# A shared scores bank returned by its last reader, buffers counted, values behind four pairs' queries, the small loads held, level tiles of 32x32

## The chip, the cores and the metric

The kernel runs on one core of one Trainium2 chip. The number that counts is the time of one execution on the device, in microseconds (us). Before the change the median of three runs is 564.14 us.

## The reference, cut to what matters

One layer of a decoder trunk on 512 positions of width 1024, batch 1, all in float32:

```python
h = rmsnorm(x, norm1_w)
proj = h @ w_in                    # one projection, columns split among three groups
y_a = dilated_attention(aq, ak, av, bias_a)      # A: 6 heads of 64, three (window, dilation) branches
y_b = gla(bq, bk, bv, br, ba, ...)               # B: 4 heads, keys of 32, values of 64, decay gate of rank 16
y_c = moba_attention(cq, ck, cv, bias_c)         # C: 6 heads of 64, blocks of 256, top 3 of the past
mix = concatenate([y_a, y_b, y_c])
x = x + mix @ w_out
h2 = rmsnorm(x, norm2_w)
x = x + square(relu(h2 @ w_ff1)) @ w_ff2         # w_ff1 is 1024 x 4096
return rmsnorm(x, final_norm_w)
```

At 512 positions the three dilated branches of a query reach known sets of keys, so the kernel computes A as one softmax with an added table (relative bias and the logarithm of how many branches hold the distance), and C as one causal softmax with a bias: two blocks of 256 leave nothing to choose. In B, log a = log_sigmoid(a_lr @ w_a2 + b_a) / 16 is the decay, and o_t = q_t S_t with S_t = diag(a_t) S_(t-1) + k_t v_t.

## The kernel before

**Precision.** Weights and activations of the large products are split into a high and a low part in the rounded float32 format that TensorE multiplies in one pass (fp32r). `wh` is the rounded weight, made on ScalarE, `wl = w - wh`, made on VectorE; `xh` and `xl` are the same for the activations. A product is three matmuls: high by high, high by low, low by high. A matmul in plain fp32 is two passes and leaves two records in the trace.

**Stages.** The projection runs in pieces. `first()` (L753) streams eight slices of x (`xT`, 128 x 512) and of `w0` (128 x 528), and sums B's queries and keys (`bq`, `bk`) and B's values with the gate's low-rank input (`av`) over them. `qk_proj(p)` (L1183) makes queries and keys of a pair p of heads, A's and C's twelve heads being six pairs: two weight pieces per pair, 24 products each, into `qkps`. `v_proj()` (L1114) makes A's and C's values, `out_proj()` (L1349) the output projection, `ffn()` (L1570) the feed-forward part in units; these three use seven products of half-size sums in place of eight (`f1X`, `f2Z` and the like are their accumulators). `main()` (L1640) runs them in this order, with the values behind the queries of two pairs.

Beside them go `row_scale()` (L636): sums of squares over the slices, `rsp`, then `ss`, `rstd`, `diag` on VectorE and `rps` on TensorE, which spreads 1/rms along the rows. `bias_table()` (L666) multiplies the relative biases by a one-hot table: `vt`, then `vals`, written to DRAM as `tab`. `gla()` (L770): `alps` transposes the gate input to `alT`, `zps` multiplies it by w_a2, and a scan gives the decay. The 128 x 128 causal blocks of B are computed by levels: at level L (64, 32, ... 1), queries in the later half of each group of 2L positions meet keys in the earlier half, with a decay measured from the point between. The level products `lp` are four heads in four strips of 32 rows of TensorE, for four chunks n of 128 positions: the 128 columns of keys are loaded as weights, 64 columns of queries stream, for every level, and the entries outside a level are thrown away afterwards: levels 64 and 32 by ScalarE copies of the valid rows, the rest by a masked copy on VectorE. `attention()` (L952) makes the scores of one pair (`sps`), with 64 rows of TensorE for each head; `softmax()` (L1055) reads a bank of scores into `P` and normalises; `values()` (L1025) transposes P and multiplies it by the values.

**What sets the order.** The order of instructions on every engine is worked out when the program is built. Each part is a stream of operations; `Plan` (L107) holds a clock for each engine, gives every operation an estimated cost (L43 on), and issues next the operation with the earliest start, ties by the stream's priority and age. A stream can wait for an event, or take one of a resource. Resources are the eight PSUM banks (two `mm` for the large products, two `s`, two `pt`, one `o`, one `g`), the weight buffers, and so on. `slot()` (L227) hands out 52 small SBUF buffers of 2 KB per partition (`SLOTS`); the plan doesn't know about these, so an operation whose buffer is not yet free waits on the chip although the plan saw no wait.

`SCORES` and `HOMES` are tables: into which blocks the scores of a pair's four query blocks are cut, and which banks each takes. Pairs 2, 3 and 4 run query block 3 first (six matmuls) and then the three others (eighteen). Query block 0 shares the bank of block 2 (`SHARED`); the bank is given back by the softmax of the block that is last in the list.

`load_small()` (L624) issues the small constants on GpSimd's queue once the second slice's `xh` is made: `cst` (identity, flip and mask), `smask`, `hsel`, `rb` (relative bias), `bav`, `wa2`, `oneh`, then `lmask` and `gw`. All helpers record their operations on one line, L136 (L171 after the change), so the rows are told apart by their tiles' names.

Of the kernel before, what the change touches and what calls it, by code (L numbers as in the profile page):

```python
# [19 lines left out]
NT = S // 128  # L20
# [11 lines left out]
SCORES = {0: ((3, 2, 0, 1),), 1: ((3, 2, 0, 1),), 2: ((3,), (2, 0, 1)), 3: ((3,), (2, 0, 1)), 4: ((3,), (2, 0, 1)), 5: ((3,), (2, 0), (1,))}  # L32
SHARED = {(p, 0): 2 for p in range(6)}
HOMES = {0: {3: ('s', 's'), 2: ('o', 'g'), 1: ('pt', 'pt')}, 1: {3: ('s', 's'), 2: ('o', 'g'), 1: ('pt', 'pt')}, 2: {3: ('s', 's'), 2: ('s', 's'), 1: ('o', 'g')}, 3: {3: ('s', 's'), 2: ('s', 's'), 1: ('o', 'g')}, 4: {3: ('s', 's'), 2: ('s', 's'), 1: ('o', 'g')}, 5: {3: ('s', 's'), 2: ('s', 's'), 1: ('s', 's')}}
O_ORDER = (0, 1, 3, 5, 2, 4, 6)
# [4 lines left out]
class Op:  # L40


    def __init__(self, eng, method, args, kw):  # L43
# [14 lines left out]
        if eng == "tensor":  # L58
# [4 lines left out]
            elif wide and inner[-1].shape[0] == 32:  # L63
                self.cost = 0.031
# [9 lines left out]
        elif eng == "vector":  # L74
# [4 lines left out]
            self.cost = 0.075 + n * rate / 1000  # L79
        elif eng == "gpsimd":  # L80
            self.cost = 0.15 + n * (0.9 if method == "memset" else 2.1) / 1000
        if method == "dma_start":
            self.cost = 0.9 if "accum_op" in kw else 0.06
            self.rate = 170e3 if "accum_op" in kw else 320e3
            self.size = 4 * n * args[0].shape[0]

# [20 lines left out]
class Plan:  # L107
# [5 lines left out]
    def __init__(self, nc, resources):  # L113
        self.nc = nc
        self.clock = dict(tensor=0.0, scalar=0.0, vector=0.0, gpsimd=0.0, sync=0.0, dge=0.0, dma=0.0)
# [7 lines left out]
    def spawn(self, gen, prio=0):  # L123
        self.streams.append(dict(gen=gen, prio=prio, item=None, at=self.now, sent=None, n=len(self.streams)))
# [7 lines left out]
    def start(self, op, at):  # L132
        return max([self.clock[op.eng], at] + [self.ready.get(n, 0.0) for n in op.ins])

    def issue(self, op, at):
        getattr(getattr(self.nc, op.eng), op.method)(*op.args, **op.kw)  # L136
        t = self.start(op, at)
        end = t + op.cost
# [4 lines left out]
        if op.method == "dma_start":  # L143
            if "accum_op" in op.kw:
                self.clock["dma"] = max(self.clock["dma"], end + 1.0) + op.size / op.rate
                end = self.clock["dma"] + 3.0
            else:
# [3 lines left out]
        for n in op.outs:  # L151
            self.ready[n] = max(self.ready.get(n, 0.0), end + self.LAT)
        return end
# [7 lines left out]
    def run(self):  # L161
        while self.streams:
            cand, moved = None, False
            for st in list(self.streams):
                while True:
                    if st["item"] is None:
                        try:
                            moved = True
# [27 lines left out]
                    if cand is None or (t, st["prio"], st["n"]) < cand[:3]:  # L196
                        cand = (t, st["prio"], st["n"], st, o)
# [15 lines left out]
def hybrid_block_kernel(ctx: ExitStack, tc: tile.TileContext, xT_d, x_d, w0_d, wv_d, wqk_d, wo_d, w1_d, w2_d,  # L213
                        nw_d, ba_d, wa2_d, gw_d, fw_d, rb_d, oh_d, cst_d, lm_d, out_d):
# [8 lines left out]
    plan = Plan(nc, dict(BANKS, raw=3, rawv=5, rawo=8, w=WPAIRS, big=BIGS, raw2=3, part=5, lev=4, xp=2))  # L223
# [3 lines left out]
    def slot(name, dt=F32, shape=(128, 512)):  # L227
        return sp.tile(list(shape), dt, name=name, tag="slot", bufs=SLOTS)
# [34 lines left out]
    rb, wa2, gw = misc[:, 0:128], misc[:, 128:256], misc[:, 256:512]  # L263
    lmask = slot("lmask", I32, (128, len(LEVELS), 64))
    oneh = [slot("oneh", shape=(128, 320)) for _ in range(2)]
    alT = slot("alT", shape=(128, 512))
    xT = [slot("xT") for _ in range(KT)]
    tab = dr.tile([12, 640], F32, name="tab")
    R, Rn8, ssx = slot("R"), slot("Rn8"), slot("ssx")
# [354 lines left out]
    def load_small():  # L624
        yield ("wait", ("xh", 1))
        for t, d in ((cst, cst_d[:, 0:512]), (smask, cst_d[:, 512:1024]), (hsel, cst_d[:, 1024:1028]), (rb[:34, :12], rb_d),
                     (bav, ba_d), (wa2[:16], wa2_d)):
            yield POOL.dma_start(t, d)
        for i in range(2):
            yield POOL.dma_start(oneh[i][:34], oh_d[:, i * 320:(i + 1) * 320])  # L630
        fire("consts")
        spawn(bias_table(oneh), 1)
# [33 lines left out]
    def bias_table(oneh):  # L666
        yield ("wait", "R")
        for i in range(2):
# [1104 lines left out]
```

## Time and profile before

| | |
|---|---|
| three timed runs | 564.91, 564.14, 563.35 us |
| median | 564.14 us |
| profiled execution | 565.38 us |
| its span, first to last instruction | 563.4 us |
| mean TensorE clock granted | 0.998 |
| ScalarE, VectorE, GpSimd busy | 370.9, 478.9, 68.9 us |
| moved by DMA | 96.59 MB, mean 171 GB/s |

The profile is one execution. PE is TensorE, PEld its weight loads, which overlap the matmuls, DVE is VectorE, ACT ScalarE, POOL GpSimd. A row of a group names `out<-in`, the count, busy time, the mean of one in ns, and the idle time of the engine just before with what ended it. Matmuls are pipelined, so the time of one record is longer than the distance from its start to the next one's; distances are what counts. The span leaves out some 2 us around the first and the last instruction.

### The profile page before, as it was taken

What the parts mean: (1) busy time and instruction counts of PE and PEld (TensorE: products, weight loads), DVE (VectorE), ACT (ScalarE), POOL (GpSimd) and SP (SyncE); (2) the same over time, 40 slices, a digit from 0 to 9 for tenths busy, and PEclk for the clock granted to TensorE, in tenths of its full rate; (3) what the DMA queues carried; (4) which work ended last, traced back from release to release, by engine and by line L of the source; (5) the groups of instructions that cost most, each with busy time, mean ns of one, the idle gap of its engine ahead of it and who ended that gap; (6) DMA issues with size and microseconds to landing.
All of it is one profiled execution on the core that took longest, in us unless ns stands there. A gap on an engine that the chain in (4) does not pass through costs nothing.

```text
span 563.4 us, 9466 instructions
## 1 busy us (share of the span) xinstructions
PE 552.7 (98%) x3513; PEld 477.5 (85%) x3513; DVE 478.9 (85%) x872; ACT 370.9 (66%) x661; POOL 68.9 (12%) x90
## 2 busy tenths in 40 slices
PE   8999999999999999999999999999999999999994
PEld 7977887886876767899987899988999888999884
DVE  4899899998668988999699995799957899867984
ACT  5755745787665866989766476855377654679553
POOL 5003110001000002111121010120020110102102
PEclk9999999999999999999999999999999999999999
DMA  8944596195134756992989439686388694385803
GB/s 280 403 139 116 91 267 165 33 390 140 38 47 136 244 137 126 266 273 65 282 202 200 157 80 290 188 149 192 113 177 272 121 219 146 89 211 113 149 37 113
DMA packets 29949, 96.59 MB, mean 171 GB/s; under 512 B 3648, under 2 KB 3690, under 8 KB 29904
## 3 DMA queue, kind: packets, MB, share of 16 engines
q0 software_dynamic: 9456, 33.53, 32.9%
q1 hardware_dynamic: 20160, 62.20, 31.0%
q8 instruction: 27, 0.44, 0.3%
q10 hardware_dynamic: 288, 0.27, 0.1%
q14 instruction: 18, 0.15, 0.1%
HBM read 93.86 MB, written 2.13 MB: 170 GB/s over the span
## 4 chain that ended last, share of the span: by engine, by line
PE 81%; DVE 11%; DMA 3%; ACT 2%; issue 2%; SPq 0%; DVEq 0%; ACTq 0%; POOLq 0%
PE f2X L136 14%; PE f1X L136 13%; PE qkps L136 9%; PE f1Z L136 8%; PE f2Z L136 7%; PE ops L136 7%; PE f1Y L136 4%; PE vps L136 4%; DMA wraw<-in_w 3%; PE f2Y L136 3%; DVE wl L136 3%; PE ptp L136 3%; PE po L136 2%; PE sps L136 2%; DVE P L136 2%
## 5 line engine op out<-in xcount | busy, mean ns | idle before, releaser
L136 DVE TENSOR_TENSOR wl<-wraw,wh 128x1024 fp32r<-128x1024 f32 (+2 forms) x174 | 192.1, 1111 | 37.0 <-ACT wh L136 36.8
L136 ACT ACTIVATE wh<-wraw 128x1024 fp32r<-128x1024 f32 (+2 forms) x173 | 164.2, 966 | 58.2 <-DMA wraw<-in_w 14.6
L136 PE MATMUL f1X<-yp,wh 128*128 128x256 f32 x512 | 92.7, 283 | 0.0
L136 PEld LDWEIGHTS f1X<-yp,wh 128*128 128x128 f32 x512 | 80.1, 192 | 0.3
L136 POOL DMA_DIRECT2D wraw<-in_w x46 | 40.5, 947 | 270.0 <-DVE wl L136 220.1
L136 PE MATMUL f1X<-yp,wl 128*128 128x256 f32 x256 | 72.4, 283 | 0.0
L136 PE MATMUL f2X<-wh,Al 128*128 128x512 f32 (+1 forms) x132 | 50.6, 383 | 0.0
L136 PE MATMUL f2X<-wh,Ah 128*128 128x512 f32 (+1 forms) x132 | 50.5, 383 | 0.0
L136 PE MATMUL f2X<-wl,Ah 128*128 128x512 f32 (+1 forms) x132 | 50.5, 383 | 0.0
L136 PEld LDWEIGHTS f1X<-yp,wl 128*128 128x128 f32 x256 | 49.1, 192 | 0.0
L136 PE MATMUL f1Z<-yp,wh 128*128 128x256 f32 x256 | 46.3, 283 | 0.0
L136 ACT ACTIVATE h<-h 128x512 f32<-128x512 f32 x56 | 34.7, 625 | 10.5 <-DVE h L136 9.9
L136 PE MATMUL qkps<-xh,wh 128*128 128x512 f32 x96 | 40.3, 420 | 0.0
L136 PEld LDWEIGHTS f1Z<-yp,wh 128*128 128x128 f32 x256 | 39.9, 192 | 0.0
L136 ACT ACTIVATE Ah<-h 128x512 fp32r<-128x512 f32 x40 | 24.1, 620 | 21.5 <-DVE h L136 21.5
L136 PE MATMUL qkps<-xh,wl 128*128 128x512 f32 x96 | 37.6, 392 | 0.0
L136 PE MATMUL qkps<-xl,wh 128*128 128x512 f32 x96 | 37.4, 390 | 0.0
L136 PE MATMUL f1Z<-yp,wl 128*128 128x256 f32 x128 | 36.2, 283 | 0.0
L136 ACT ACTIVATE P<-P,mn 128x512 f32<-128x512 f32 (+3 forms) x48 | 26.4, 552 | 7.9 <-DVE mn L136 7.9
L136 DVE TENSOR_TENSOR Al<-h,Ah 128x512 fp32r<-128x512 f32 x40 | 26.9, 688 | 3.2 <-ACT Ah L136 3.0
L136 PEld LDWEIGHTS f2X<-wh,Ah 128*128 128x128 f32 x132 | 24.8, 188 | 4.9
L136 PEld LDWEIGHTS f2X<-wl,Ah 128*128 128x128 f32 x132 | 24.8, 188 | 4.8
(264 smaller groups left out, 1221.0 us busy)
## 6 DMA issues: line engine op xcount, KB each, us to landing
wraw<-in_w SPq DMA_DIRECT2D x66, 512.0 KB, 5.3
wraw<-in_w POOLq DMA_DIRECT2D x46, 512.0 KB, 6.8
wraw<-in_wqk SPq DMA_DIRECT2D x12, 512.0 KB, 6.7
wraw<-in_wv SPq DMA_DIRECT2D x10, 512.0 KB, 6.9
wraw<-in_wv POOLq DMA_DIRECT2D x8, 512.0 KB, 5.4
wraw<-in_wo SPq DMA_DIRECT2D x8, 512.0 KB, 10.1
wraw<-in_wo POOLq DMA_DIRECT2D x8, 512.0 KB, 5.5
nb<-tab SPq DMA_DIRECT2D x12, 256.0 KB, 4.9
```

The source lines that it names most:

```text
L136: getattr(getattr(self.nc, op.eng), op.method)(*op.args, **op.kw)
```

## The change

**The planner counts small buffers.** The program is planned twice: a first pass without emitting counts how often each buffer of `slot()` is used (`own`, `count`), and the second pass knows from that when a buffer comes free, and delays an operation that has no free one. Some buffers are kept in reserve for the level products and the feed-forward part. Costs of a few VectorE operations are set anew, and each stream that begins before 180 us gets a random addition to its priority, from a fixed seed.

```diff
     def start(self, op, at):
-        return max([self.clock[op.eng], at] + [self.ready.get(n, 0.0) for n in op.ins])
+        t = max([self.clock[op.eng], at] + [self.ready.get(n, 0.0) for n in op.ins])
+        if self.uses is not None:
+            new = len({n for n in op.outs + op.ins if n in self.key and n not in self.left})
+            if new:
+                if op.outs[0].startswith(("nb", "P0", "P1", "P2", "th")):
+                    new += self.reserve
...
+                t = max(t, sorted(self.slots)[new - 1]) if new <= len(self.slots) else math.inf
+        return t
```

**A shared bank goes back with its last reader**, whichever that is in the issued order. Pair 3's scores become one block, a pair takes one of three `pair` resources before its scores and returns it with its values, and the two heads' short rows share a buffer (`A2`).

```diff
-SCORES = {0: ((3, 2, 0, 1),), 1: ((3, 2, 0, 1),), 2: ((3,), (2, 0, 1)), 3: ((3,), (2, 0, 1)), 4: ((3,), (2, 0, 1)), 5: ((3,), (2, 0), (1,))}
+SCORES = {0: ((3, 2, 0, 1),), 1: ((3, 2, 0, 1),), 2: ((3,), (2, 0, 1)), 3: ((3, 2, 0, 1),), 4: ((3,), (2, 0, 1)), 5: ((3,), (2, 0), (1,))}
...
         yield DVE.tensor_tensor_reduce(P, s, nb, 1.0, 3e38, OP.add, OP.min, mn)
-        if last:
-            give(last)
+        home, readers = last
+        readers.remove(key[2])
+        if not readers:
+            give(home)
```

**Values behind four pairs' queries.** `main()` and the list of weight pieces use `VPOS = 4` where they had 2.

**The small loads are held** behind the third slice of x, by a one-column copy on GpSimd that reads it:

```diff
     def load_small():
         yield ("wait", ("xh", 1))
+        yield POOL.tensor_copy(x2c, xT[2][:, :1])
```

**One fp32r matmul for vt and for zps.** High and low parts stand below one another along the contracted side: 96 rows for `vt` (before 34), 48 for `zps` (before 16). The loads bring the copies, two operations on ScalarE round them into `stat`, two on VectorE subtract; three on VectorE build `al3` from `alr`, and the four transposes `alps` have 48 rows in place of 16.

```diff
+    def stacked():
+        yield ACT.activation(rbs[:96, :12], rb[:96, :12], AF.Copy)
+        yield DVE.tensor_tensor(rbs[64:96, :12], rb[64:96, :12], f32(rbs[64:96, :12]), op=OP.subtract)
+        yield ACT.activation(wa2s[:48], wa2[:48], AF.Copy)
+        yield DVE.tensor_tensor(wa2s[32:48], wa2[32:48], f32(wa2s[32:48]), op=OP.subtract)
+        fire("stacked")
...
-            yield PE.matmul(vt[:, :320], rb, oneh[i], start=True, stop=True)
+            yield PE.matmul(vt[:, :320], rbs, oneh[i], start=True, stop=True)
...
-        yield PE.matmul(zps, wa2, alT, start=True, stop=True)
+        yield PE.matmul(zps, wa2s, alT, start=True, stop=True)
```

**Level tiles of 32x32.** For levels 64 and 32 only the valid part is multiplied: 32 columns of keys as weights, against 64 columns of queries (level 64) or 32 (level 32), twice per head and chunk. The results of both levels stand below one another in the bank, and ScalarE's copies read them from there. The levels from 16 down keep their form.

```diff
                 for n in range(NB):
+                    if L >= 32:
+                        for j in range(2):
+                            for h in range(4):
+                                c = kq[32 * h:32 * h + 32, n * 128:(n + 1) * 128]
+                                key, q0, q1 = (32 * j, 64, 128) if L == 64 else (64 * j, 64 * j + 32, 64 * j + 64)
+                                r0, c0 = 64 * i + 32 * j, n * 64 + q0 - 64 if L == 64 else n * 32
+                                ops.append(PE.matmul(lp[h][r0:r0 + 32, c0:c0 + q1 - q0], c[:, key:key + 32], c[:, q0:q1],
+                                                     start=True, stop=True))
+                        continue
```

**What moves.** GpSimd's queue at the start of the program, before the change: the memsets, then the small loads in a row (`in_rb`, `in_wa`, `in_oh`, `in_lm` and `in_gw` are the arrays in DRAM).

```order
L136 MEMSET misc 128x128 x2
L136 MEMSET oneh 128x320 x2
L136 MEMSET alT 128x512
L136 DMA cst<-in_cst 128x512
L136 DMA smask<-in_cst 128x512
L136 DMA hsel<-in_cst 128x4
L136 DMA misc<-in_rb 34x12
L136 DMA bav<-in_ba 128x1
L136 DMA misc<-in_wa 16x128
L136 DMA oneh<-in_oh 34x320 x2
L136 DMA lmask<-in_lm 128x448
L136 DMA misc<-in_gw 128x256
```

The same place after the change:

```order
L171 MEMSET alT 128x512
L171 COPY x2c<-xT 128x1
L171 DMA cst<-in_cst 128x512
L171 DMA smask<-in_cst 128x512
L171 DMA hsel<-in_cst 128x4
L171 DMA misc<-in_rb 96x12
L171 DMA bav<-in_ba 128x1
L171 DMA misc<-in_wa 48x128
L171 DMA oneh<-in_oh 96x320 x2
L171 DMA lmask<-in_lm 128x448
L171 DMA misc<-in_gw 128x256
```

A copy that reads the third slice of x stands ahead of all small loads, whose order is as it was.

VectorE's queue at the end of the projection's slices, before, from the last `wl` of a slice to `diag` (`xs` and `xsl` are half-size sums of x for the values, the 1024-wide `wl` belong to the pairs' queries and keys):

```order
L136 SCALAR_TENSOR_TENSOR xs<-xT,nw,xs 128x256
L136 TENSOR_SCALAR ss<-rsp 128x4
L136 SCALAR_TENSOR_TENSOR xs<-xT,nw,xs 128x256 x2
L136 TENSOR_TENSOR wl<-wraw,wh 128x1024
L136 TENSOR_TENSOR tmp_392<-rstd 128x4
L136 SCALAR_TENSOR_TENSOR xs<-xT,nw,xs 128x256
L136 SCALAR_TENSOR_TENSOR tmp_392<-tmp_392,ss 128x4
L136 TENSOR_TENSOR wl<-wraw,wh 128x1024
L136 SCALAR_TENSOR_TENSOR rstd<-tmp_392,rstd 128x4
L136 TENSOR_TENSOR xsl<-xs,xsh 128x1024
L136 TENSOR_SCALAR nrstd<-rstd 128x4
L136 TENSOR_SCALAR diag<-cst,rstd 128x128 x4
```

and after, where one more `wl` of 1024 columns and two `xs` stand ahead of the first row, behind the last slice's `wl`:

```order
L171 SCALAR_TENSOR_TENSOR xs<-xT,nw,xs 128x256 x2
L171 TENSOR_TENSOR wl<-wraw,wh 128x1024
L171 TENSOR_SCALAR ss<-rsp 128x4
L171 TENSOR_TENSOR xsl<-xs,xsh 128x1024
L171 TENSOR_TENSOR tmp_416<-rstd 128x4
L171 TENSOR_TENSOR wl<-wraw,wh 128x1024
L171 SCALAR_TENSOR_TENSOR tmp_416<-tmp_416,ss 128x4
L171 SCALAR_TENSOR_TENSOR xs<-xT,nnw,xs 128x256
L171 SCALAR_TENSOR_TENSOR rstd<-tmp_416,rstd 128x4
L171 SCALAR_TENSOR_TENSOR xs<-xT,nnw,xs 128x256
L171 TENSOR_SCALAR nrstd<-rstd 128x4
L171 TENSOR_SCALAR diag<-cst,rstd 128x128 x4
```

So two `wl` and three more `xs` stand ahead of `ss`, and one `wl`, one `xsl` and two `xs` between `ss` and `diag`.

ScalarE's queue in the second half of the projection's slices, after the change (`sq` are the squares for the row sums; before it, no `stat` stood between `xh`, `wh` and `sq`):

```order
L171 ACTIVATE wh<-wraw 128x528
L171 ACTIVATE stat<-misc 96x12
L171 ACTIVATE xh<-xT,nw 128x512
L171 ACTIVATE wh<-wraw 128x528
L171 ACTIVATE stat<-misc 48x128
L171 ACTIVATE sq<-xT 128x512
L171 ACTIVATE xh<-xT,nw 128x512
```

The two roundings of the small loads stand ahead of the `xh` of the sixth and of the seventh slice.

On TensorE the level products of the first block (`lp`, with the query products before it and the value products behind it) read before:

```order
L136 MATMUL qkps<-xh,wl 128x512
L136 MATMUL vps<-wh,xh 128x512
L136 MATMUL vps<-wh,xl 128x512
L136 MATMUL vps<-wl,xh 128x512
L136 MATMUL lp<-kq 128x64 x32
L136 MATMUL vps<-wh,xh 128x512
```

and after:

```order
L171 MATMUL qkps<-xh,wl 128x512
L171 MATMUL lp<-kq 32x64 x32
L171 MATMUL lp<-kq 32x32 x32
L171 MATMUL qkps<-xh,wh 128x512
L171 MATMUL qkps<-xl,wh 128x512
```

The block has twice the matmuls, of 32 rows of output, and stands among the queries of the third and fourth pair and no longer among the values.

More of the change, by code (lines that the diff above doesn't have):

```diff
@@ L79, in __init__ @@
             self.cost = 0.075 + n * rate / 1000
+            if method == "tensor_tensor_scan":
+                self.cost = 1.13
+            elif method == "copy_predicated":
+                self.cost = 0.58 if args[0].shape[-1] == 1 else 0.33
+            elif any(a.shape[-1] == 1 and n > 4 for a in inner) or method == "scalar_tensor_tensor":
+                self.cost += 0.055
         elif eng == "gpsimd":
@@ L152, in issue @@
             self.ready[n] = max(self.ready.get(n, 0.0), end + self.LAT)
+        for n in held if self.uses is not None else ():
+            self.left[n] -= 1
+            if self.left[n] == 0:
+                self.slots.append(end + self.LAT)
         return end
@@ L262, in hybrid_block_kernel @@
     ident, flip, bmask = cst[:, 0:128], cst[:, 128:256], cst[:, 256:512]
-    rb, wa2, gw = misc[:, 0:128], misc[:, 128:256], misc[:, 256:512]
+    rb, wa2, gw = misc[:, 0:16], misc[:, 128:256], misc[:, 256:512]
+    stat = slot("stat", F32R)
+    rbs, wa2s = stat[:, 0:128], stat[:, 128:256]
     lmask = slot("lmask", I32, (128, len(LEVELS), 64))
-    oneh = [slot("oneh", shape=(128, 320)) for _ in range(2)]
-    alT = slot("alT", shape=(128, 512))
+    oneh = [slot("oneh", F32R, (128, 320)) for _ in range(2)]
+    alT = slot("alT", F32R, (128, 512))
     xT = [slot("xT") for _ in range(KT)]
     tab = dr.tile([12, 640], F32, name="tab")
+    x2c = consts.tile([128, 1], F32)
     R, Rn8, ssx = slot("R"), slot("Rn8"), slot("ssx")
@@ L625, in load_small @@
         yield ("wait", ("xh", 1))
[L626 to L627 removed]
+        yield POOL.tensor_copy(x2c, xT[2][:, :1])
+        for t, d in ((cst, cst_d[:, 0:512]), (smask, cst_d[:, 512:1024]), (hsel, cst_d[:, 1024:1028]), (rb[:96, :12], rb_d),
+                     (bav, ba_d), (wa2[:48], wa2_d)):
             yield POOL.dma_start(t, d)
         for i in range(2):
[L630 removed]
+            yield POOL.dma_start(oneh[i][:96], oh_d[:, i * 320:(i + 1) * 320])
         fire("consts")
+        spawn(stacked(), 1)
         spawn(bias_table(oneh), 1)
@@ L667, in bias_table @@
         yield ("wait", "R")
+        yield ("wait", "stacked")
         for i in range(2):
@@ L776, in gla @@
         alr = small("alr", (128, NT, 16))
+        al3 = sp.tile([128, NT, 48], F32R, name="al3", tag="al3", bufs=1)
         for t in range(NT):
             yield DVE.tensor_scalar(alr[:, t, :], acc_v[t][:, 256:272], rstd[:, t:t + 1], None, op0=OP.mult)
+        yield DVE.tensor_copy(al3[:, :, 0:16], alr)
+        yield DVE.tensor_tensor(al3[:, :, 16:32], alr, f32(al3[:, :, 0:16]), op=OP.subtract)
+        yield DVE.tensor_copy(al3[:, :, 32:48], alr)
         for t in range(NT):
@@ L783, in gla @@
         alps = bank("g", "alps")
-        yield [PE.transpose(alps[:16, t * 128:(t + 1) * 128], alr[:, t, :], ident) for t in range(NT)]
-        yield DVE.tensor_copy(alT[:16], alps[:16, :])
+        yield [PE.transpose(alps[:48, t * 128:(t + 1) * 128], f32(al3[:, t, :]), ident) for t in range(NT)]
+        yield DVE.tensor_copy(alT[:48], alps[:48, :])
         give("g")
@@ L988, in attention @@
                 yield ops
+                readers = {}
+                for qb in qbs:
+                    for e in range(2):
+                        readers.setdefault((SHARED.get((p, qb), qb), e), []).append(qb)
                 for qb in qbs:
@@ L1051, in values @@
             yield ops
+            for p in ps_:
+                give("pair")
             for p, po, r in zip(ps_, pos, "og"):
@@ L1653, in hybrid_block_kernel @@
             piece(("x", k + 1), xT_d[k + 1])
-    for p in range(2):
+    for p in range(VPOS):
         for i in range(2):
@@ L1657, in hybrid_block_kernel @@
     piece("v", None)
-    for p in range(2, 6):
+    for p in range(VPOS, 6):
         for i in range(2):
@@ L1669, in start @@
         yield DVE.memset(eps, EPS)
-        for z in (rb, wa2, *oneh, alT):
-            yield POOL.memset(z, 0.0)
+        for z in (rb, stat[:, :256], *oneh, alT):
+            yield POOL.memset(z if z.dtype == F32 else f32(z), 0.0)
         yield DVE.tensor_scalar(nw2, nw[:, 1], -0.5, None, op0=OP.mult)
@@ L1694, in hybrid_block_kernel @@
     plan.run()
+    if not emit:
+        raise Counted(plan)
 def _bucket(n):
```

115 lines of the change are left out of this document (80 added, 35 removed).

## The prediction

> **What bounds the kernel now.** I read the page first, its part 1, for the engines' shares.
>
> ```profile
> span 563.4 us, 9466 instructions
> PE 552.7 (98%) x3513; PEld 477.5 (85%) x3513; DVE 478.9 (85%) x872; ACT 370.9 (66%) x661; POOL 68.9 (12%) x90
> ```
>
> TensorE is busy in all but 11 us. That alone could hide matmuls that crawl, so next I asked what TensorE waited for (total, times, longest, in us).
>
> ```profile
> PE av L136 <- ACT wh L136: 1.2, 2, 0.7
> ...
> PE f2Z L136 <- ACT wh L136: 0.4, 1, 0.4
> PE zps L136 <- DVE alT L136: 0.2, 1, 0.2
> ```
>
> Besides the warm-up matmuls' first wait these come to 1.8 us, two thirds of it in the input projection. The chain of work that ended last (start, us, what) gives the pace of a matmul when nothing is in its way, and the busy times by stretch (length, then busy us and instructions of PE, PEld, DVE, ACT) show which other engine is full.
>
> ```profile
> 44.11 12.28 PE qkps L136 x54
> 304.13 16.32 PE f2X L136 x72
> ...
> 45.00:57.00 12.00, 12.00 (x54) 9.64 (x52) 12.00 (x22) 6.71 (x11) 2.91 (x6) 1.00 0.58 140
> 57.00:95.00 38.00, 38.00 (x364) 31.82 (x364) 36.04 (x73) 23.88 (x42) 4.35 (x5) 1.00 0.71 165
> 132.00:170.00 38.00, 38.00 (x232) 28.47 (x230) 27.35 (x87) 26.03 (x67) 1.75 (x2) 1.00 0.34 72
> 400.00:480.00 80.00, 80.00 (x519) 73.43 (x518) 66.83 (x79) 48.66 (x64) 8.80 (x10) 1.00 0.68 173
> ```
>
> A 512-column product takes 12.28/54 = 0.227 us both at 44 us and at 304 us, at a granted clock of 1.00. So TensorE is the bound, and time is won only by fewer TensorE passes or fewer of its waits. VectorE is the second bound: full from 45 to 57 us, 2 us of slack in the 38 after that, 10.6 us of slack from 132 to 170. Moving the values behind four pairs' queries shifts work between these stretches. TensorE had no gap in either, so the move itself is worth nothing on TensorE; it can only cost or spare waits.
>
> **The start.** TensorE's rows in order of time show the two gaps of the projection; then ScalarE's rows and the small loads that GpSimd issues (start, us, engine, operation; in brackets the idle time before it), and the loads' sizes with the time from issue to landing.
>
> ```profile
> 7.50 0.40 PE L136 MATMUL bk<-xh,wl 128*128 128x512 f32 x1
> 8.55 0.76 PE L136 MATMUL av<-wh,xh 128*128 128x272 f32 x4 [0.66 <-ACT wh L136]
> ...
> 9.38 0.40 PE L136 MATMUL bk<-xh,wh 128*128 128x512 f32 x1
> 9.62 0.66 PE L136 MATMUL av<-wh,xl 128*128 128x272 f32 x4
> ...
> 11.32 0.40 PE L136 MATMUL bk<-xh,wl 128*128 128x512 f32 x1
> 12.24 0.77 PE L136 MATMUL av<-wh,xh 128*128 128x272 f32 x4 [0.53 <-ACT wh L136]
> ...
> 2.10 0.74 POOL L136 DMA_DIRECT2D cst<-in_cst  x1
> 4.97 0.52 POOL L136 DMA_DIRECT2D misc<-in_wa  x1
> 9.39 0.73 ACT L136 ACTIVATE xh<-xT,nw 128x512 fp32r<-128x512 f32 x1 [0.36 <-DMA xT<-in_xT]
> 11.55 0.64 ACT L136 ACTIVATE wh<-wraw 128x528 fp32r<-128x528 f32 x1 [1.44 <-DMA wraw<-in_w]
> ...
> xT<-in_xT SPq DMA_DIRECT2D x8, 256.0 KB, 7.3
> ...
> cst<-in_cst POOLq DMA_DIRECT2D x1, 256.0 KB, 5.5
> ...
> misc<-in_wa POOLq DMA_DIRECT2D x1, 8.0 KB, 6.4
> ```
>
> From bk to the next av it is 0.24 us without a gap, and 1.05 and 0.92 us at the two gaps: 0.81 + 0.68 = 1.49 us. Both gaps end with a slice of the weights landing while ten small loads, issued from 2.10 us, share the DMA engines. In the changed kernel a copy on GpSimd waits for the third slice of x, and the small loads stand behind it, so the first weight slices have the engines to themselves. The cst table alone is as large as a slice of x. I take both gaps as gone: **-1.49 us** (bounds 0 and -1.49).
>
> What is late next? VectorE's ss, rstd and diag, which rps waits for.
>
> ```profile
> 24.91 0.95 PE L136 MATMUL rsp<-ones,ssx 128*128 128x2 f32 x8
> 25.90 0.16 DVE L136 TENSOR_SCALAR ss<-rsp 128x4 f32<-128x4 f32 x1 [2.55 <-PE rsp L136]
> ...
> 22.56 1.05 ACT L136 ACTIVATE wh<-wraw 128x1024 fp32r<-128x1024 f32 x1
> 26.77 1.22 DVE L136 TENSOR_TENSOR wl<-wraw,wh 128x1024 fp32r<-128x1024 f32 x1
> 30.86 0.87 DVE L136 TENSOR_SCALAR diag<-cst,rstd 128x128 f32<-128x128 f32 x4
> 32.03 1.02 PE L136 MATMUL rps<-diag,ones 128*128 128x512 f32 x2
> ```
>
> VectorE sat idle 2.55 us before ss. In the new order two whole wl and three more xs stand in that place. The total of bytes is the same, so the weights of the first queries land no sooner: ScalarE makes the first wh at about 22.6 and the second 1 us later, the second wl ends near 25.8, and ss comes when it came before. Behind ss the new order has one xsl and one wl (about 1.15 each back to back), two xs of a quarter of their width (0.4 each), small ones (0.4) and diag (0.87): 4.4 us, so diag is ready near 30.5. TensorE reaches rps at 32.03 - 1.49 - 0.68 = 29.86, the 0.68 because rps is placed three products earlier. That is a new wait of **+0.7 us** (bounds 0 and 2).
>
> **One pass in place of two.** vt and zps run in fp32 and leave two records per matmul; with rounded high and low parts stacked along the contracted side they are one fp32r pass.
>
> ```profile
> 41.89 0.39 PE L136 MATMUL qkps<-xh,wl 128*128 128x512 f32 x1
> 42.45 1.12 PE L136 MATMUL zps<-alT,misc 128*128 128x512 f32 x2 [0.17 <-DVE alT L136]
> 43.41 0.70 PE L136 MATMUL vt<-oneh,misc 128*128 128x320 f32 x2
> ...
> 43.57 0.54 PE vt L136 x2
> ```
>
> vt: 0.54 to 0.227 x 320/512 = 0.14 us, twice: -0.80. zps: 43.41 - 42.45 = 0.96 to 0.227: -0.73. Together **-1.53 us**, all on TensorE. The wait ahead of zps (42.45 - 41.89 = 0.56 against 0.23) is 0.33 us; in the new order VectorE goes from the last al3 to alT through three xs and two vals (0.4 us each) and alT itself, 2.6 us, while TensorE goes from alps to zps through the four transposes (0.4), vt and nine products, 2.6 us too: they meet. I take **-0.33** (bounds +0.6 and -0.33). The two stat operations on ScalarE and two on VectorE (about 0.2 us each, like ss) fall where ScalarE waits for slices to land, and cost nothing while that wait is there; otherwise 0.4.
>
> **32x32 level tiles.** The first block of level products.
>
> ```profile
> 57.07 1.94 PE lp L136 x64
> 59.02 2.95 PE vps L136 x12
> ```
>
> Today 64 passes in 1.94 us, 0.030 us each, each loading 128 columns of weights. Afterwards there are 128 passes that load 32 columns and stream at most 64. By loaded columns the block is half, 0.97 us; by passes it is double, 3.88. Four passes in four row strips go at once today, 0.12 us per four, which is the pace of a 128-column load and not of the stream of 64; so the first end is the nearer, and I take **-0.97** (bounds -0.97 and +1.94). The Trainium skill, "TensorE: Matmul & The Clock Gate", section "LDWEIGHTS", has a load last its columns / 1.2 ns: 27 ns for 32 columns, with 32 groups of four an estimate of 0.85 us. The same page, section "Wait — 56ns, not 53.3ns?", speaks against the change: starts of matmuls never come closer than about 25 ns. No run here shows which holds for tiles this small; today's mean of 30 ns fits both.
>
> **One block of scores fewer.** Pair 3's scores run as one block of 24, not 6 and 18. Entering the half-array form and leaving it costs: behind lp, twelve vps take 2.95 us where 12 x 0.227 = 2.72, so 0.23 for leaving, and I put as much for entering: **-0.45 us** (bounds 0 and -0.6). Against it, this block takes all six banks at once, and the second level blocks follow VectorE's evacuations closely; TensorE, some 3 us earlier, finds VectorE with 2 us of slack in 57 to 95. I set **+0.5 us** of waits there (bounds 0 and 2). That a bank goes back with its last reader, and that buffers are counted, changes only the planner's order: no instruction comes or goes, 0 us.
>
> **Behind 230 us** the order is nearly the same. The tightest place is the first feed-forward unit:
>
> ```profile
> 252.86 10.10 PE f1Z L136 x84
> 262.99 0.69 DVE yp L136
> ...
> 266.61 8.74 DMA wraw<-in_w
> ...
> 298.44 5.70 PE f2Z L136 x24
> ```
>
> The chain to f2Z leaves TensorE at 263 us, so it starts earlier with TensorE, and the 0.4 us wait stays. After 304 us there is no wait to win or lose.
>
> **Sum:** -1.49 + 0.7 - 1.53 - 0.33 - 0.97 - 0.45 + 0.5 = -3.57 us. The profiled execution took 565.38 us (its span 563.4 and 2.0 around it), which would become 561.8; the three timed runs have a median of 564.14, 1.2 below it, so the forecast is **560.6**.
>
> **Rivals.**
> - *The new waits do not come.* Then -4.77: 559.4. For it: VectorE is relieved by moving the values, whose wl and xs work was densest from 57 to 95. Against it: the count for rps above.
> - *VectorE takes over until 95 us.* It gets five small operations more, its work up to the level blocks is otherwise the same, and the stretch from 45 to 57 had no idle time. Then the one-pass and tile gains turn into waits, and what is left is the scores block and half of the 1.49 us, by which the projection feeds VectorE earlier: -1.2, 562.9. Against it: four pairs' queries give TensorE 24 x 0.227 = 5.4 us for each piece of weights, on which VectorE spends one wl and two operations of half its width, about 2.4.
> - *Small tiles are bound by starts.* By rows: if 128 passes cost 0.025 us each, the block is 3.2 us, 1.26 more than now in place of 0.97 less: -1.34, 562.8. This is what the Trainium skill's 25 ns, cited above, would do.
> - *ScalarE stands behind a small load.* Its second stat operation waits for wa2 and stands ahead of xh and wh of the seventh slice. wa2 was issued at 4.97 and took 6.4 us, so it landed at 11.4, 9.3 us after the first small issue at 2.10. The third slice of x lands now at 9.4 and may land from 8 us on; then wa2 lands at 17 to 18.7. TensorE needs that slice near 22.3 and ScalarE about 2.2 us to prepare it, so from a landing at 20.1 each us is a us lost, and at 25.5 the kernel is slower than before: 565.9. It would take loads twice as slow as now.
>
> **How the numbers follow.** Forecast 0.52, no new waits 0.17, VectorE 0.15, starts of small tiles 0.12, the small load 0.04. The range from 559.0 to 563.7 takes in the first four with their bounds where they do not add up. A measurement of this kernel can tell 0.3% (1.7 us) from no change; faster than 562.4 is the forecast with most of its bounds, the second case, and the better edges of the next two: 0.75. Within 0.3%: 0.20. Slower: 0.05.
>
> **What would show it.** Right: no gap before av at the second and third slice; vt and zps with one record each; the first lp block near 1 us; a wait of rps for diag under 1 us; 0.227 us per product everywhere else. Wrong: a first lp block over 2 us, waits of lp or sps for VectorE that sum to over 2 us, ScalarE idle before stat for us on end, or a wait of f2Z that has grown by the gain.

## The result and the profile after

| | median | runs | ratio to before, 95% interval |
|---|---|---|---|
| before | 564.52 us | 563.35 to 565.06 | |
| after | 560.87 us | 560.74 to 561.15 | 0.9939 (0.9921 to 0.9956) |

The change makes the kernel 0.6% faster, 3.65 us by the medians; 560.6 was forecast. The profile's page of after, its span and engines:

```profile
span 559.4 us, 9572 instructions
PE 550.0 (98%) x3574; PEld 478.1 (85%) x3574; DVE 479.7 (86%) x872; ACT 373.7 (67%) x668; POOL 69.1 (12%) x91
```

What TensorE waited for in after (total, times, longest, in us):

```profile
PE rps L171 <- DVE diag L171: 1.1, 1, 1.1
PE warm L171 <- DVE ones L171: 1.1, 1, 1.1
PE lp L171 <- DVE attn L171: 0.3, 2, 0.2
```

The three waits of before (av, f2Z, zps) are gone; one at rps has come, and 0.3 us at the level products `lp`. So far this reads like the forecast. The same view hides more, though: a wait at the head of a block whose first records overlap the record ahead isn't in it. I therefore set the ends of TensorE's records in the two traces side by side, at points that both programs pass with the same work done:

| | before | after | change, us | forecast, us |
|---|---|---|---|---|
| end of the last slice (bk) | 30.80 | 29.36 | -1.44 | -1.49 |
| rps, from the record ahead to its end | 0.86 | 2.20 | +1.34 | +0.7 |
| vt twice, and zps with its wait | 2.37 | 0.52 | -1.85 | -1.86 |
| first level block | 1.94 | 1.31 | -0.63 | -0.97 |
| the three other level blocks | 5.16 | 6.78 | +1.62 | in +0.5 |
| all else up to the first f1Y, by subtraction | | | -1.40 | -0.45, and in +0.5 |
| f2Z of the first unit | 11.57 | 10.88 | -0.69 | 0 |
| last matmul to the end of the span | 7.50 | 6.57 | -0.93 | 0 |

With -0.04 elsewhere that is the span's 563.40 - 559.38 = 4.02 us. The two profiled executions (565.38 and 561.15 us) differ by more than the medians do, so 0.4 us of this table is the draw of these two. The total was met; three of its terms were 0.3, 0.6 and more than 1 us too good, and gains that were not forecast, in the last three rows, filled the hole.

**One pass.** TensorE's rows in order of time at vt and zps (start, us, operation):

```profile
35.52 0.31 PE L171 MATMUL vt<-oneh,stat 128*128 128x320 f32 x1
35.66 0.40 PE L171 MATMUL qkps<-xh,wh 128*128 128x512 f32 x1
...
38.98 0.39 PE L171 MATMUL zps<-alT,stat 128*128 128x512 f32 x1
39.20 0.39 PE L171 MATMUL qkps<-xh,wh 128*128 128x512 f32 x1
```

One record each, the next start 0.14 and 0.22 us later, and no wait ahead of zps.

**rps.** TensorE, then ScalarE and VectorE, in after; in brackets the idle time before and what ended it:

```profile
29.66 0.40 PE L171 MATMUL qkps<-xh,wl 128*128 128x512 f32 x1
31.16 1.10 PE L171 MATMUL rps<-diag,ones 128*128 128x512 f32 x2 [1.10 <-DVE diag L171]
...
15.44 0.21 ACT L171 ACTIVATE stat<-misc 96x12 fp32r<-96x12 f32 x1 [2.06 <-DMA misc<-in_rb]
15.55 0.71 ACT L171 ACTIVATE xh<-xT,nw 128x512 fp32r<-128x512 f32 x1
...
15.68 0.16 DVE L171 TENSOR_TENSOR stat<-misc,stat 32x12 fp32r<-32x12 f32 x1 [0.78 <-ACT stat L171]
...
26.51 0.15 DVE L171 TENSOR_SCALAR ss<-rsp 128x4 f32<-128x4 f32 x1
...
30.14 0.86 DVE L171 TENSOR_SCALAR diag<-cst,rstd 128x128 f32<-128x128 f32 x4
```

ScalarE stands 2.06 us behind the load of rb, which the hold has made late (without the hold, run 2, it doesn't wait there), with xh of the sixth slice queued behind it; VectorE stands behind ScalarE, has no idle stretch over 0.2 us between 16.9 and 30 us, and finishes diag at 31.0. From the start of ss, 26.51, that is 4.5 us, where 4.4 were forecast; ss itself comes 0.6 us after the forecast's 25.9.

**The level blocks.** TensorE's first and second block in after, with ScalarE's copies between them and the weight load that waits for the copies, and then VectorE's masked copies and the two pieces at which the fourth block waits:

```profile
52.90 1.38 PE L171 MATMUL lp<-kq 32*32 32x64 f32 x128
54.20 0.50 PE L171 MATMUL qkps<-xh,wh 128*128 128x512 f32 x1
...
59.34 1.13 ACT L171 ACTIVATE attn<-lp 32x128 f32<-32x128 f32 x4
59.87 2.65 PE L171 MATMUL lp<-kq 32*128 32x64 f32 x64
...
60.52 1.86 PEld L171 LDWEIGHTS lp<-kq 32*128 32x128 f32 x58 [0.28 <-ACT attn L171]
...
72.87 3.79 DVE L171 COPY_PREDICATED attn<-lmask,lp 128x256 f32<-128x256 int32 x8 [1.66 <-PE lp L171]
...
76.23 0.40 PE L171 MATMUL lp<-kq 32*128 32x64 f32 x2 [0.16 <-DVE attn L171]
76.80 1.07 PE L171 MATMUL lp<-kq 32*128 32x64 f32 x26 [0.17 <-DVE attn L171]
```

The first block does 128 passes in 1.31 us, 0.010 us each. The second starts at 59.87, while ScalarE empties its banks until 60.47, and takes 0.64 us more than its work. The fourth goes bank by bank as VectorE's masked copies end.

**The end.** DMA of 7 us near the end, before (555 to 562 us) and then after (552 to 559): q14, the queue that fetches instructions, with one packet of 8 KB (count, MB, share), and the last store on ScalarE's queue (size, us from issue to landing). In that stretch of after q14 has no packet.

```profile
q14 instruction: 1, 0.01, 0.3%
...
out<-xw ACTq DMA_DIRECT2D x1, 256.0 KB, 3.7
```

```profile
out<-xw ACTq DMA_DIRECT2D x1, 256.0 KB, 2.8
```

### The profile page after: what moved, and what is told of

Same layout as the page of the kernel before. It is cut to its first block, busy times and chain, and to the rows that moved or that the text cites. A ratio compares the mean times of both kernels' runs of the same rounds, so it can differ in the third digit from the quotient of the medians.

```text
span 559.4 us, 9572 instructions
## 1 busy us (share of the span) xinstructions
PE 550.0 (98%) x3574; PEld 478.1 (85%) x3574; DVE 479.7 (86%) x872; ACT 373.7 (67%) x668; POOL 69.1 (12%) x91
## 4 chain that ended last, share of the span: by engine, by line
PE 95%; DVE 2%; ACT 1%; issue 1%; ACTq 0%; DVEq 0%
PE f1X L171 16%; PE f2X L171 15%; PE qkps L171 11%; PE f1Z L171 8%; PE f2Z L171 8%; PE ops L171 7%; PE vps L171 7%; PE f1Y L171 4%; PE f2Y L171 4%; PE ptp L171 3%; PE po L171 2%; PE sps L171 2%; PE av L171 2%; PE lp L171 1%; PE op L171 1%; PE bk L171 1%
## 5 line engine op out<-in xcount | busy, mean ns | idle before, releaser
L171 PEld LDWEIGHTS f2X<-wh,Al 128*128 128x128 f32 x132 | 24.8, 188 | 4.7
```

## The experiments

"Orders kept" means that the planner's order is untouched on every engine, so that only the named instructions differ. The profiled execution of each kernel gives the ends of records; its time is one execution where no interval stands beside it.

**1. The hold alone, in the kernel before (orders kept).**

```diff
         yield ("wait", ("xh", 1))
+        nc.gpsimd.tensor_copy(x2c, xT[2][:, :1])
```

> The kernel before with the hold alone: one GpSimd copy of a column of the third x slice ahead of the small loads, all engines' orders otherwise as before. Theory A (small loads take the DMA engines from the weight slices): the waits of av for wh (0.66 and 0.53 us) fall under 0.2 us in sum and bk of the last slice ends near 29.4 instead of 30.80; VectorE's diag doesn't follow by as much, so rps, which has no wait before, waits 0.3 to 1.2 us for it. Time 0.3 to 1.2 us under the kernel before (563 to 564). Rival B (the gaps are the pace of the weight loads themselves): the two waits stay, and time stays within 0.3 us. Rival C (the hold is worth its full 1.49): no wait of rps, time 1.5 us under.

564.64 us against 564.71 for before on the same chip. TensorE's waits:

```profile
PE warm L136 <- DVE ones L136: 1.1, 1, 1.1
PE f2Z L136 <- ACT wh L136: 0.4, 1, 0.4
```

The waits of av for wh are gone, and none came at rps (theory A's second half fell: in this order VectorE stands idle 5.0 us ahead of ss). The last slice ends at 29.97, 0.83 earlier than in the profile of before and not 1.4. The time, one execution each, doesn't show it, so no theory is met whole.

**2. The changed kernel without the hold (orders kept).**

```diff
-        yield POOL.tensor_copy(x2c, xT[2][:, :1])
```

> The changed kernel without the hold, orders as in it. Theory A: av waits for wh again, 1.2 to 1.5 us in sum, and the wait of rps for diag (1.1 us by the table of waits) shrinks to 0 to 0.3, because diag hangs on the weights of the first queries and not on TensorE; rps ends within 0.4 us of 32.25, and the time is within 0.6 us of the changed kernel: the hold's gain is taken back at rps. Rival: diag follows TensorE, the rps wait stays near 1.1, rps ends near 33.7, and the time is 1.4 us longer.

560.89 us. The last slice ends at 29.64, and rps at 31.98.

```profile
PE rps L171 <- DVE diag L171: 0.6, 1, 0.6
PE lp L171 <- DVE attn L171: 0.3, 2, 0.2
PE av L171 <- ACT wh L171: 0.3, 1, 0.3
```

Half of the rps wait went with the hold, and one of the two waits of av came back, and the time is that of the changed kernel. What the hold won, 0.28 us at the last slice here, was taken back at rps, as A says. Its sizes missed: av lost 0.3 us and not 1.2 to 1.5, so 1.49 was one execution's figure. The rps wait doesn't go whole either: ScalarE no longer waits for rb, yet VectorE comes to ss at 26.23 and ends diag at 30.74.

**3. Wide level tiles in the changed kernel (orders kept).**

```diff
                     if L >= 32:
-                        for j in range(2):
...
+                        for h in range(4):
...
+                            op = PE.matmul(o.rearrange("p (m l) -> p m l", l=L), c, q, start=True, stop=True)
+                            op.cost, op.mode = 0.032, (True, True)
```

ScalarE's copies read the valid rows from their old places again.

> The changed kernel with levels 64 and 32 multiplied as before (128 columns of keys as weights, 64 of queries, 64 passes for 128), same orders. First lp block 1.94 us in place of 1.31. Theory A: ScalarE's copies and with them the second lp block move by the same 0.6, so nothing behind absorbs it: 0.6 us longer. Rival B: the second lp block (2.58 us, of which 0.64 is a wait) waits for ScalarE, whose pace doesn't depend on this block; then its wait shrinks and the time is within 0.1 us.

562.24 us. Its first and its second block:

```profile
53.44 2.01 PE L171 MATMUL lp<-kq 32*128 32x64 f32 x64
61.05 2.52 PE L171 MATMUL lp<-kq 32*128 32x64 f32 x64
```

First block 1.94 by ends of records, second 2.45 for 2.58. From the end of rps to the end of the span it takes 527.66 us, the changed kernel 527.13: the tiles are worth 0.5 us, 0.63 less the 0.1 that the second block's wait gives back. Theory A. (The rest of what this execution is longer than the changed kernel's profiled one, 561.15, stands ahead of rps's end, at 32.80 us for 32.25.)

**4. vt and zps in two passes in the changed kernel (orders kept).**

```diff
-            yield PE.matmul(vt[:, :320], rbs, oneh[i], start=True, stop=True)
+            two = PE.matmul(vt[:, :320], f32(rbs), f32(oneh[i]), start=True, stop=True)
```

and zps likewise.

> The changed kernel with vt and zps multiplied in plain fp32 (two passes) from the same stacked operands, same orders. vt 0.54 us each for 0.14, zps 0.96 for 0.23: TensorE reaches the qkps behind zps 1.5 us later. Theory A: the waits behind (second lp block 0.64, fourth 0.98) hang on blocks that TensorE itself ended, so they stay, and the time is 1.5 us longer. Rival B: they are paced by VectorE and ScalarE alone and shrink by what TensorE loses: 0 to 0.5 us longer.

562.99 us, and 528.68 us from rps to the end against 527.13: 1.55 us, the 1.53 of the forecast; by ends of records 1.45 of it stand up to the end of zps. The second block still takes 2.59 and the fourth 2.25. The waits of the level blocks hang on blocks that TensorE itself ended, so nothing absorbs work taken off ahead of them. Theory A.

**5 and 6. Where an instruction fetch falls.** Ten one-column memsets on VectorE at the start of the kernel before, and four in the changed kernel:

```diff
         yield DVE.memset(eps, EPS)
+        for _ in range(10):
+            nc.vector.memset(idle, 0.0)
```

> The kernel before with ten one-column memsets more on VectorE at the very start (into a tile that nobody reads), all else in the same order. In its trace the last store on ScalarE's queue lands 3.7 us after its issue, in the changed kernel 2.8, and only in the kernel before an instruction fetch of 8 KB lies between the packets of the last stores. Theory A (VectorE's next block of instructions is fetched just then, and one DMA engine does it ahead of the store's packets): ten instructions more bring that fetch forward, ahead of the last store; the store lands in 2.8 us, and the span ends 6.6 us behind TensorE's last matmul in place of 7.5. Rival B (the store is slow for another reason, such as the addresses): 3.7 and 7.5 stay. TensorE's times up to its last matmul as before, within the 0.8 us by which the start varies.

> The changed kernel with four one-column memsets more on VectorE at the start: VectorE then has as many records as in the kernel before (1090 in place of 1086). Theory A (instruction fetch): the fetch falls among the last stores again, the store lands in 3.7 us and the span ends 7.5 us behind the last matmul in place of 6.6: 0.9 us longer than the changed kernel. Rival B: 2.8 and 6.6 stay.

The last store of the first, then of the second:

```profile
out<-xw ACTq DMA_DIRECT2D x1, 256.0 KB, 2.8
```

```profile
out<-xw ACTq DMA_DIRECT2D x1, 256.0 KB, 3.7
```

From the last matmul to the end of the span: 6.53 us with ten more in before (7.50 without), 7.49 with four more in after (6.57 without). In the traces the fetch starts 2.9 us ahead of the end of the span in before and with four more in after; with ten more in before it starts 8.0 us ahead, and in after 1.1 us behind the end. Theory A holds both ways: 0.9 of the 3.65 us come from the count of VectorE's instructions. The time of the first kernel, 563.99 us in one execution, lies within the spread of before on that chip (563.97 to 565.52, median 564.51) and doesn't show it by itself. The second kernel took 565.15 us, though, 4.3 and not 0.9 more. The rest stands at rps. ScalarE's wait for rb, TensorE's rows behind it, and the window from 28 to 36 us (length, busy us and count of PE, PEld, DVE, ACT, POOL, granted clock, DMA share, GB/s):

```profile
ACT stat L171 <- DMA misc<-in_rb: 3.5, 1, 3.5
...
32.59 1.69 PE L171 MATMUL rps<-diag,ones 128*128 128x512 f32 x2 [2.31 <-DVE diag L171]
34.94 0.63 PE L171 MATMUL qkps<-xh,wl 128*128 128x512 f32 x1
35.36 0.63 PE L171 MATMUL qkps<-xh,wh 128*128 128x512 f32 x1
...
28.00:36.00 8.00, 5.69 (x20) 3.80 (x19) 7.00 (x20) 4.86 (x10) 0.00 (x0) 0.81 0.88 351
```

The load came 1.4 us later than in the changed kernel's profile, rps waited 2.3 us, and behind that wait the granted clock fell: products started 0.42 us apart in place of 0.227 until 36.5 us. Wait and clock together put zps at 42.47, 3.1 us later than in the changed kernel. So the small load's place is a risk too, and not only the 1.1 us of one profile.

**7. rps six products later** (a delay of 1.4 us for it in the planner; one row moves on TensorE and one on VectorE).

```diff
         yield ("wait", "first")
+        yield ("delay", 1.4)
         rps = bank("mm", "rps")
```

> The changed kernel with rps six query products later on TensorE (the planner delays it by 1.4 us; one place on TensorE and one on VectorE move, nothing else). Theory A (TensorE waits 1.1 us at rps for diag, while products lie ready behind it): the wait goes; diag and so rps end when they did, and six products more are done by then, 1.3 us of work: everything behind is 1.3 us earlier, time 559.5. Rival B (what follows hangs on VectorE, which is full until 57 us): the wait comes back at alps, zps or the first level block, and the time is within 0.3 us of the changed kernel.

560.69 us (560.29 to 561.06), ratio 0.9931 (0.9914 to 0.9947): no different from the changed kernel, where theory A had 559.5. The wait at rps is gone (0.86 us from the record ahead to its end); TensorE's wait is now this:

```profile
PE alps L171 <- DVE al L171: 0.5, 1, 0.5
```

From the last slice's end to zps it takes 9.35 us in place of 10.01: half of the wait is won, the other half comes back at alps, which waits for VectorE. Rival B, in that the time stays; half of the wait was won in the trace all the same.

**8. The same, and the second and fourth level block later by the planner**, 0.8 and 1.2 us ahead of `yield ops`.

> As the run before, and the second and the fourth block of level products are also put later by the planner (0.8 and 1.2 us), since in the changed kernel they take 2.58 and 2.26 us with waits, against 1.94 and 1.28 before; the order behind 60 us changes with it. Theory A: these waits go too, 0.64 and 0.98: time 558 to 558.5. Rival B: the new order behind has waits of its own, which the planner's costs don't see: 559.5 or more.

590.57 us (586.67 to 590.85), ratio 1.0445 (1.0411 to 1.048). The second block takes 1.94 and the fourth 1.05, as theory A has it, but the planner orders the rest anew, and that order stalls. Its longest waits, and then its windows from 110 to 140 and from 200 to 245 us (length, busy us and count of PE, PEld, DVE, ACT, POOL, granted clock, DMA share, GB/s):

```profile
PE ptp L171 <- DVE P L171: 5.9, 1, 5.9
PE ptp L171 <- ACT th L171: 4.9, 3, 4.1
...
110.00:140.00 30.00, 23.78 (x122) 18.71 (x121) 22.10 (x65) 21.61 (x44) 2.63 (x3) 0.87 0.72 214
200.00:245.00 45.00, 38.89 (x198) 26.58 (x197) 28.32 (x77) 28.55 (x65) 1.80 (x3) 0.84 0.27 80
```

TensorE idles 6.2 of the 30 us, and the clock granted falls to 0.87 and 0.84; the changed kernel has 1.00 in both windows. The loss is there twice, as idle time and as slower matmuls. Rival B.

**9. The roundings of the small loads behind R** (two stat operations on ScalarE, two on VectorE; all else kept).

```diff
-        yield ACT.activation(rbs[:96, :12], rb[:96, :12], AF.Copy)
...
     def bias_table(oneh):
         yield ("wait", "R")
         yield ("wait", "stacked")
+        for op in late4 if emit else ():
+            getattr(getattr(nc, op.eng), op.method)(*op.args, **op.kw)
```

> The changed kernel with the four small operations that round wa2 and the biases (two stat on ScalarE, two on VectorE) put behind R in place of among the slices; nothing else moves. Theory A (the wait of rps comes from them: ScalarE waits 2.1 us for the held load of rb ahead of xh, so VectorE starts the wl of the first queries late and comes late to ss and diag): ScalarE's wait goes, diag is ready 1.0 to 1.5 us earlier, the wait of rps falls to 0 to 0.3, and all behind is earlier by as much: span behind zps as before, time 559.4 to 560.0. Rival B (diag hangs on the landing of the first queries' weights): diag stays within 0.4 us of 31.0, the rps wait stays, time within 0.3 us of the changed kernel.

561.07 us (560.09 to 561.39), ratio 0.992 (0.9907 to 0.9934), no different from the changed kernel; theory A had 559.4 to 560.0. In the trace ss starts at 25.21 us for 26.51, VectorE ends diag at 29.5 in place of 31.0, and TensorE doesn't wait at rps:

```profile
28.64 0.87 DVE L171 TENSOR_SCALAR diag<-cst,rstd 128x128 f32<-128x128 f32 x4
...
30.64 1.02 PE L171 MATMUL rps<-diag,ones 128*128 128x512 f32 x2
```

So the wait at rps came from the roundings that stand behind the small load, as A says, and A's time missed: alps waits 0.4 us for VectorE, the last slice ended at 30.11 in this execution, and zps ends at 39.32, as in the changed kernel.

**10. The same, rps three products later, and the second level block three products later** (the block is held back where instructions are emitted, and rps by a delay of 0.7 us in the planner; beyond these, one `wl` moves on VectorE, and all else keeps its order).

```diff
+            for o in ops:
+                o.behind = {0: 0, 2: 3, 4: 0, 6: 3}[l0]
             yield ops
```

> As the run before, and rps three query products later, and the second block of level products three query products later (0.7 us), where it waited 0.64 us for ScalarE's copies out of its banks. Theory A: the second block takes 1.94 us in place of 2.58 and all behind gains another 0.6: 558.8 to 559.4. Rival B: what is late next is VectorE, and the wait moves to the third or fourth block: no gain over the run before.

559.81 us (559.54 to 560.08), ratio 0.9905 (0.9891 to 0.9918): the fastest of all, its interval just below that of the changed kernel. The second block:

```profile
59.94 2.01 PE L171 MATMUL lp<-kq 32*128 32x64 f32 x64
```

1.94 by ends of records for 2.58, the third 1.99, the fourth 2.22 (it stayed in its place). Theory A for the block; its time, 558.8 to 559.4, was 0.4 us too good.

**11. Pair 3 in two blocks in the changed kernel**, by the rows of SCORES and HOMES of before.

> The changed kernel with pair 3's scores in blocks of 6 and 18 as in the kernel before; the planner orders anew around it. Theory A: one more entry into the half-array form and one more way out (0.28 to 0.31 and 0.20 us each in the trace), 0.5 us longer behind 140 us, and nothing else. Rival B: the block of 24 that takes all six banks at once had cost waits, so that without it TensorE is 0.3 to 1 us earlier. Rival C: the new order has other waits, and it can't be told.

567.04 us in one execution, the first f1Y starting 5.5 us later. Rival C: the planner's order changes on every engine that computes, and the waits are those of the new order:

```profile
PE sps L171 <- DVE mn L171: 1.3, 1, 1.3
...
PE ops L171 <- ACT th L171: 0.6, 1, 0.6
```

What one block fewer is worth by itself can't be read from it.

**12. Number 10 without the hold (orders kept).**

> The run stat_late_defer without the hold, all orders the same. In the profiles so far bk of the last slice ends at 29.36 to 30.18 us in ten kernels with the hold (mean 29.83) and at 29.64, 30.17 and 30.80 in three without it (mean 30.20); and rps, which took the start's gain back in the changed kernel, waits no longer. Theory A (the hold is worth the difference of these means): 0.4 us longer than stat_late_defer, 560.2. Rival B (worth the 1.44 us by which the two first profiles differ): 561.2. Rival C (worth nothing, the start varies by chance): 559.6 to 560.0.

560.8 us (560.16 to 561.66), ratio 0.9933 (0.992 to 0.9947), against 559.54 to 560.08 with the hold: 1.0 us, between theories A and B. With the roundings moved the hold pays in time. The one profiled execution (560.31 us) doesn't show where: the last slice ends at 29.07 without the hold, the earliest of all, but then alps and rps wait for VectorE,

```profile
PE alps L171 <- DVE al L171: 0.6, 1, 0.6
...
PE rps L171 <- DVE diag L171: 0.2, 1, 0.2
```

and zps ends at 39.00, against 38.76 with the hold. The times spread over 1.5 us in place of 0.5, and one profile of a spread is one draw. Where the 1.0 us is lost stays open.

## Why the prediction was right, and where not

- **What bounds the kernel**: right. TensorE is busy in 550.0 of 559.4 us, and the two edits behind rps with the orders kept moved the end by what they did to TensorE, to 0.1 us (runs 3 and 4).
- **The start, -1.49**: measured -1.44 in the two profiled executions, and that was luck. The hold removes a wait that differs from one execution to the next: bk of the last slice ended at 29.36 to 30.18 us in ten kernels with it (mean 29.83), at 29.07, 29.64, 30.17 and 30.80 in four without (mean 29.92). The profile of before is the latest of them all. One row of one execution was taken for the size of a wait on a DMA landing. An early last slice wasn't worth its time either, because VectorE sets when alps and zps can run: it ended 0.9 us earlier in run 12 than in run 10, and zps 0.24 later.
- **The new wait at rps, +0.7**: right in kind, +1.34 in size. The step that failed is "fall where ScalarE waits for slices to land, and cost nothing while that wait is there", and with it "ss comes when it came before": the first stat waits itself, 2.06 us (up to 3.5), for the load that the hold delays, and ss comes at 26.51 in place of 25.9. In run 9, with the roundings elsewhere, it comes at 25.21 and the wait at rps is gone. This is the mechanism of the rival "ScalarE stands behind a small load" with rb in the place of wa2, and its point of decision was put too late (20.1 us, where rb's rounding ran at 15.4): TensorE doesn't see it through the slice's xh, but through VectorE's later diag. The wait at rps is not a loss of time of the same size, though: taking it away (runs 7 and 9) left the time as it was, since alps waits for VectorE next.
- **vt and zps, -1.53 - 0.33**: right, -1.85 for -1.86, and 1.55 of passes alone by run 4.
- **32x32 tiles, -0.97**: right in kind, -0.63. The rival of starts at 0.025 us, a price that no row of this case had, fell, with 1.31 us where it gave 3.2. A group of four passes takes 41 ns (1.31 us for 32 groups), against 121 with loads of 128 columns (1.94 us for 16): about a third, not a quarter. By the loading rule of the Trainium skill, "TensorE: Matmul & The Clock Gate", section "LDWEIGHTS", the estimate was 0.85 us for the block.
- **Waits of the later level blocks, in +0.5**: too small, +1.62. That they "follow VectorE's evacuations closely" was written down and then priced with VectorE's slack of 2 us in 57 to 95. That slack is an average; the second block waits for ScalarE's copies and the fourth for eight masked copies in a row. So the second block's wait isn't one for VectorE, as the term had it. Runs 8 and 10 show that it goes when query products are put ahead of the block.
- **One block of scores fewer, -0.45**: right by the records, -0.40: the blocks themselves went from 0.90 + 1.41 to 2.11 us, and one way out of the half-array form (0.20) went. Run 11 couldn't isolate it. The other 1.0 us of that row of the table was not forecast. Half of it is at ptp, where TensorE waits for P (120 ptp records took 14.78 us, now 14.28), in pieces too small for the view of waits; the rest isn't traced. No run takes back the place of the values, the counting of buffers or the bank's return alone, so which of them won this 1.0 us is open.
- **f2Z, "the 0.4 us wait stays"**: wrong, it went, -0.69. In the queue of GpSimd's weight loads around the first feed-forward unit, before and then after, what the loads waited for differs:

```profile
POOL wraw L136 <- ACT h L136: 22.1, 2, 15.0
```

```profile
POOL wraw L171 <- ACT h L171: 3.9, 1, 3.9
```

  The claim that the order behind 230 us is nearly the same was made from TensorE's rows; GpSimd's loads stood otherwise. That this came from the counting of buffers is possible; no run shows it alone.
- **The end, 0**: not foreseen, -0.93, shown by runs 5 and 6, and by the place of the packet in their traces, to be an instruction fetch.

So the forecast was right for its middle terms and lucky in its sum: about 2 us too good at rps and the level blocks, and 2.6 us of gains that it didn't see. Of its own signs, the wait at rps was just over the 1 us that it allowed (1.1), and ScalarE did stand idle before stat "for us on end" (2.06), a sign named for being wrong; they showed which term had failed although the sum came out. Two small readings were off without changing it: the bytes of the small loads were not the same (each `oneh` load grew from 42.5 to 120 KB), and in the rival of the small load 5.4 us on 560.6 are 566.0, not 565.9.

## What to carry to other kernels

When a small load is delayed to clear the way for large ones, look for every instruction that reads it and what is queued behind that instruction; here two operations of 0.2 us stood 2 us behind such a load and made VectorE's diag, and with it rps, late. Measure a wait that ends with a DMA landing in several executions before putting it into a sum, and compare traces between points with the same work done, since waits of 0.1 to 0.3 us are missing from a list of waits. After a wait is taken away, ask what is late next: runs 7 and 9 moved a wait and won no time, and run 10 won 1 us by moving two more things. In a kernel whose order a planner makes, test an edit with the order kept: two edits that let it plan anew cost 6 and 30 us for reasons of their own.

## What the runs showed of the hardware

- Passes over 32x32 tiles, four row strips side by side, came 10 ns apart on average, 128 in 1.31 us. The Trainium skill, "TensorE: Matmul & The Clock Gate", section "Wait — 56ns, not 53.3ns?", has a floor of about 25 ns between starts; it doesn't bind passes in different strips here.
- An instruction fetch of 8 KB among the packets of the last store delayed its landing by 0.9 us (3.7 for 2.8). The fetch moved away with ten VectorE instructions more at the start of the program, and came back with four in the other kernel. The Trainium skill, "Runtime: NRT & Kernel Launch", section "Instruction fetch mechanics", calls the cost of going from one block of instructions to the next mostly hidden. Here, at the end of the program, 0.9 us of it showed, as a later store.
- Idle TensorE costs twice. Behind one wait of 2.3 us the granted clock was 0.81 over 8 us (run 6), and over the stretches of 30 and 45 us in run 8 it was 0.87 and 0.84. Run 8 has three slow pieces: 0.53 from 132 to 143 us, behind a wait of 5.9 us; 0.53 from 197 to 208, behind one of 4.1; and 0.51 from 221 to 228, behind waits of 3.0 and 1.8. Behind the one wait of 1.1 us in the changed kernel it stayed at 1.00. The Trainium skill, "TensorE: Matmul & The Clock Gate", section "HAM oscillation — how this bites in real kernels", puts the limit at gaps of over some 3.4 us. The first two pieces agree with that; the third, and run 6, came behind shorter waits.
